# A Griffin and short-convolution block in fp32: split weights kept in DRAM, weight sums moved, operands split sooner, a last product by token tiles

## The chip, the cores and the metric

The kernel runs on one core of a Trainium2 chip. The metric is the device time of one execution in microseconds; 2272.66 us is the median of three runs of the kernel before (2270.35 to 2274.27). A profile of one further execution stands beside them, with its own time. The engines are TensorE (PE, with its weight loads as PEld), VectorE (DVE), ScalarE (ACT), GpSimd (POOL) and SyncE (SP), each with a queue that it works off in order; DMAs are issued here from SP and POOL, and in the changed kernel also from ACT.

## The reference

One layer, sequence 2048, width 1024, all in float32:

```python
h = rmsnorm(x, norm_mix_g)
u = h @ w_in                       # 1024 x 3584, columns: b, c, v (512 each), x_r, g (1024 each)
y_conv = gate_b * causal_dwconv(gate_c * v, conv_w)
xr = causal_dwconv(x_r, rnn_conv_w) + rnn_conv_b
y_rnn = rg_lru(xr, ...) * gelu(g)  # r, i = sigmoid(block-diagonal linear of xr); scan over time
y = concat([rmsnorm(y_conv), rmsnorm(y_rnn)])
x = x + y @ w_out                  # 1536 x 1024
h = rmsnorm(x, norm_mlp_g)
z = square(relu(h @ w_mlp_in))     # 1024 x 4096
x = x + z @ w_mlp_out              # 4096 x 1024
out = rmsnorm(x, final_norm_g)
# rg_lru: a = exp(-8 r softplus(-lambda)); h_t = a h_(t-1) + sqrt(1 - a^2) i xr
```

## The kernel before, in words

**Split operands.** Each fp32 operand of a matmul is split into two fp32r tiles: hi is a copy by ACT (L160), lo the difference by DVE (L161), both in `round_off`. A product takes three matmuls, hi x hi, hi x lo and lo x hi. Every split is thus one ACT and one DVE operation on a tile of 128 x 1024.

**Blocks and pairs.** The 2048 tokens are four blocks of 512, worked off as two pairs. In a pair come the mixers, then w_out for the first and the second block (`po`), then the first MLP product (`Up`), then the second (`Down`).

**Seven products.** From the first MLP product on, the matrix products of a pair are done in Strassen's way: seven quarter products in place of eight, numbered 1 to 7 and run in `ORDER` = 1, 2, 6, 5, 7, 3, 4, each of 24 matmuls (`block_product`, L746, or `Down.multiply`, L1023). Products 1, 2 and 4 (of `w_in`) take quarters of the weight as they are, the others sums of quarters. The mixers of the first pair (`mixers_plain`) are done plainly, since there the quarters are first loaded and split; when a unit's weights have been used, `keep_sums` makes the sums of its group and spills them to DRAM. The second pair's mixers (`mixers_blocks`) fetch for each product one quarter: a sum from DRAM (`wk<-d_wk`), or for 1, 2 and 4 the raw weight from the input (`wk<-in_w_in_dram`), four products ahead, and split it two products ahead.

**The Lru mixers.** The seven groups of columns are four Lru groups (each 256 columns of x_r and of g), two short-convolution groups and the gate b. While the products of group s run, the two units of group s - 1 go through `gate` (the small block-diagonal products `psri` on PE, L492, with two sigmoids on ACT), `scan` and `out`. A unit needs `conv` first: one tensor_scalar (L475) and three more operations on DVE, and a split into xr_hi and xr_lo. `scan` has on DVE L507, L511, L512 (a tensor_scalar, r = v + 1), L513, L515 and the scan L516, on ACT L509, L510 and L514, and a copy of the last state on POOL (L517). `out` has L521 on DVE, a spill of y on POOL's queue and a square on ACT (L526). [...]

**w_out.** `w_out_rows` takes the recurrent part of y, 256 rows at a time, fetched from DRAM and split with the gain by `split_y` (L600 on ACT, L601 on DVE); `w_out_conv` takes the convolution's part, and makes the norm for the MLP with it.

**Up and Down.** `Up` has eight slices of 512 columns with seven products each, 56 in all; operands are prepared two products ahead, results drained from PSUM, squared, combined and spilled as z on SP's queue. `Down` fetches z and w2 from DRAM four products ahead. Its sums of w2's quarters are made once, in the first pair: `w2_sums`, eight times, in the first 16 of Down's 56 products, with four loads, four DVE additions of 128 x 1024 (L976 to L979) and four spills on POOL.

**What sets the order.** In the mixers of the second pair, Up and Down PE's order is the order in which the code is written. The other engines' instructions are placed by a scheduler, and each waits in its own queue for what is ahead of it. Tiles come from pools with a fixed number of slots, 15 for weights (`wp`) and 23 for temporaries (`tp`); a DMA into a slot waits for the slot's last reader.

## Time and profile before

| | us |
|---|---|
| median of three runs | 2272.66 (2270.35 to 2274.27) |
| the profiled execution | 2272.3 |
| its span | 2270.5 |
| mean granted clock of PE | 0.973 |

| stage (us of the span) | length | PE busy | DVE busy | ACT busy | clock | DMA share |
|---|---|---|---|---|---|---|
| 60 to 360, mixers of the first pair | 300 | 300.0 | 209.8 | 154.6 | 1.00 | 0.41 |
| 360 to 520, w_out | 160 | 147.0 | 92.2 | 62.9 | 0.96 | 0.38 |
| 520 to 835, Up | 315 | 313.7 | 226.9 | 108.8 | 0.99 | 0.47 |
| 835 to 960, start of Down | 125 | 114.2 | 90.0 | 46.3 | 0.96 | 1.03 |
| 960 to 1206, rest of Down, first products | 246 | 246.0 | 162.9 | 110.0 | 1.00 | 0.58 |
| 1206 to 1424, Lru mixers of the second pair | 218 | 184.8 | 173.8 | 147.6 | 0.91 | 0.29 |
| 1424 to 1485, other mixers | 61 | 61.0 | 33.9 | 18.6 | 1.00 | 0.58 |
| 1485 to 1675, w_out | 190 | 175.0 | 123.2 | 83.9 | 0.96 | 0.32 |
| 1675 to 2257, Up and Down | 582 | 582.0 | 342.6 | 203.6 | 1.00 | 0.50 |
| 2257 to 2271, the end | 14 | 0.4 | 9.0 | 4.0 | 0.64 | 0.39 |

How to read it: a window's busy times of the engines overlap, so no row adds up to its length; what counts is which of them is missing on PE and what PE was waiting for there. The clock is the share of full speed that the profile shows as granted to PE. A row of waits names the waiting instruction and the instruction that released it, with the total, the number and the longest of the waits; a row of instructions gives line, engine, operation, output and inputs, the shapes, the count, then busy time, mean ns of one, and the idle time of the engine before them.

### The profile page before, as it was taken

The numbers are of one execution on the slowest core, as the hardware profiler recorded it, in microseconds if no ns is written. First come the engines' busy times: TensorE is split into PE (matmuls) and PEld (weight loads), VectorE is DVE, ScalarE is ACT, GpSimd is POOL, SyncE is SP. The second block draws the span as 40 slices with busy tenths as digits, with TensorE's granted clock in tenths as the row PEclk, the third lists the DMA queues.
The fourth block names the chain that finished last, engine by engine and source line by source line (L and its number), as shares of the span: only waits on it lengthen the run. The fifth ranks groups of instructions, "written<-read, shape, count | busy, mean of one in ns | idle before, by whom it ended". The sixth has DMA issues, their size and how long they took to land.

```text
span 2270.5 us, 24706 instructions
## 1 busy us (share of the span) xinstructions
PE 2165.8 (95%) x9514; PEld 1785.4 (79%) x9514; DVE 1505.4 (66%) x1726; ACT 973.6 (43%) x1222; POOL 75.5 (3%) x106
## 2 busy tenths in 40 slices
PE   6999999999999989999998888999999999999997
PEld 5888887787888878788886666877788888888886
DVE  6788744649775767676758778556687666554445
ACT  5576513425323324343546666334343333433433
POOL 0011000000000011000000101000000000000000
PEclk7999999999999999999999899999999999999999
DMA  7333545421543499986342222555115444776441
GB/s 274 130 116 125 167 148 177 162 80 48 200 160 141 160 375 413 417 337 213 131 162 70 90 94 92 175 193 176 47 72 188 158 149 176 290 294 240 158 148 75
DMA packets 174743, 398.58 MB, mean 176 GB/s; under 512 B 12832, under 2 KB 72736, under 8 KB 174624
## 3 DMA queue, kind: packets, MB, share of 16 engines
q1 hardware_dynamic: 164768, 361.33, 44.4%
q0 software_dynamic: 9856, 35.66, 4.0%
q8 instruction: 75, 1.23, 0.2%
q14 instruction: 44, 0.36, 0.0%
HBM read 281.59 MB, written 115.34 MB: 175 GB/s over the span
## 4 chain that ended last, share of the span: by engine, by line
PE 51%; DVE 5%; ACT 1%; issue 1%; DVEq 0%
PE dn L1023 22%; PE up L746 13%; PE in L746 10%; PE po L229 6%; DVE xr L516 1%; DVE w_lo L161 1%; PE psri L492 1%; DVE gi L515 0%; DVE xr L479 0%; DVE H L161 0%; ACT L514 0%; ACT w_hi L160 0%; DVE gi L521 0%; DVE x L1067 0%; ACT xr L514 0%
## 5 line engine op out<-in xcount | busy, mean ns | idle before, releaser
L746 PE MATMUL up<-H,w_hi 128*128 128x512 f32 x1792 | 554.2, 391 | 2.3 <-DVE snap L932 2.3
L161 DVE TENSOR_TENSOR w_lo<-w,w_hi 128x1024 fp32r<-128x1024 f32 x208 | 253.2, 1222 | 266.4 <-ACT w_hi L160 138.0
L746 PEld LDWEIGHTS up<-H,w_hi 128*128 128x128 f32 x1792 | 337.3, 189 | 73.0 <-ACT H L160 3.1
L1023 PE MATMUL dn<-w_lo,z_hi 128*128 128x512 f32 x896 | 350.4, 391 | 9.7 <-DVE w_lo L161 9.7
L746 PE MATMUL up<-H,w_lo 128*128 128x512 f32 x896 | 350.3, 391 | 5.2 <-DVE w_lo L161 5.2
L1023 PE MATMUL dn<-w_hi,z_hi 128*128 128x512 f32 x896 | 349.9, 391 | 0.0
L1023 PE MATMUL dn<-w_hi,z_lo 128*128 128x512 f32 x896 | 349.7, 390 | 0.0
L160 ACT CAST w_hi<-w 128x1024 fp32r<-128x1024 f32 x208 | 215.6, 1049 | 134.3 <-PE dn L1023 117.8
L746 PE MATMUL in<-H,w_hi 128*128 128x512 f32 x784 | 248.4, 399 | 16.2 <-ACT w_hi L160 16.2
L1023 PEld LDWEIGHTS dn<-w_lo,z_hi 128*128 128x128 f32 x896 | 168.9, 188 | 46.8 <-DVE w_lo L161 11.6
L160 ACT CAST z_hi<-z 128x1024 fp32r<-128x1024 f32 x112 | 117.7, 1051 | 200.7 <-PE dn L1023 158.1
L746 PEld LDWEIGHTS up<-H,w_lo 128*128 128x128 f32 x896 | 168.9, 189 | 41.2 <-DVE w_lo L161 6.0
L1023 PEld LDWEIGHTS dn<-w_hi,z_hi 128*128 128x128 f32 x896 | 168.8, 188 | 35.4 <-ACT z_hi L160 0.2
L1023 PEld LDWEIGHTS dn<-w_hi,z_lo 128*128 128x128 f32 x896 | 168.9, 189 | 35.0
L746 PEld LDWEIGHTS in<-H,w_hi 128*128 128x128 f32 x784 | 151.4, 194 | 49.0 <-ACT w_hi L160 17.5
L161 DVE TENSOR_TENSOR z_lo<-z,z_hi 128x1024 fp32r<-128x1024 f32 x112 | 136.8, 1222 | 76.2 <-issue 57.7
L161 DVE TENSOR_TENSOR w_lo<-raw,w_hi 128x1024 fp32r<-128x1024 f32 x76 | 92.8, 1223 | 125.5 <-ACT w_hi L160 84.8
L746 PE MATMUL in<-H,w_lo 128*128 128x512 f32 x392 | 156.5, 399 | 17.0 <-DVE w_lo L161 17.0
L160 ACT CAST w_hi<-raw 128x1024 fp32r<-128x1024 f32 x76 | 79.8, 1051 | 187.1 <-PE po L229 109.7
L229 PE MATMUL po<-w_hi,y_hi 128*128 128x512 f32 x384 | 123.4, 403 | 21.1 <-ACT y_hi L600 21.1
L919 ACT COPY snap<-up 128x1024 f32<-128x1024 f32 x48 | 48.7, 1014 | 193.1 <-PE up L746 193.1
L229 PE MATMUL po<-w_hi,y_lo 128*128 128x512 f32 x384 | 122.1, 400 | 0.7 <-DVE y_lo L601 0.7
(241 smaller groups left out, 3110.7 us busy)
## 6 DMA issues: line engine op xcount, KB each, us to landing
z<-d_z SPq DMA_DIRECT2D x112, 512.0 KB, 7.1
w<-in_w_mlp_out_dram SPq DMA_DIRECT2D x80, 512.0 KB, 9.4
w<-in_w_mlp_in_dram SPq DMA_DIRECT2D x64, 512.0 KB, 4.5
d_z<-snap SPq DMA_DIRECT2D x64, 512.0 KB, 2.6
w<-d_w SPq DMA_DIRECT2D x64, 512.0 KB, 4.6
raw<-in_w_out_dram SPq DMA_DIRECT2D x48, 512.0 KB, 3.5
d_z<-z SPq DMA_DIRECT2D x48, 512.0 KB, 2.6
d_w<-w POOLq DMA_DIRECT2D x32, 512.0 KB, 7.5
```

The source lines that it names most:

```text
L160: nc.scalar.copy(hi, src)
L161: V.tensor_tensor(lo, src, hi.bitcast(F32), SUB)
L229: nc.tensor.matmul(ps[:, half, :], ys[:, j, t * P : (t + 1) * P], ws[j][:, 0, half * 512 : (half + 1) * 512], start=first and i == 0, stop ...
L492: nc.tensor.matmul(ps[g][:, blk, :], ws[:, j, g, :], xs[:, blk * TB : blk * TB + TB], start=i == 0, stop=i == len(pl) - 1,)
L516: V.tensor_tensor_scan(v, r, gi, state[:, c, :], MUL, ADD)
L746: nc.tensor.matmul(ps[:, j, :], ws[:, k, j * P : (j + 1) * P], hs(k), start=i in (1, 2, 5) and k == 0 and n == 0, stop=k == 3 and n == len ...
L919: nc.scalar.copy(t, ps)
L1023: nc.tensor.matmul(ps[t // 2][:, t % 2, :], zs[:, p, t * P : (t + 1) * P], ws[:, p, :], start=i in (1, 2, 5) and a == 0 and p == 0 and n == 0,
```

## The change

- **Split quarters kept.** When a unit of `w_in` is split in the first pair, the hi and lo tiles of quarters 1, 2 and 4 are spilled to DRAM (`spill_r`, L131 of the changed kernel): six DMAs of 512 KB on SP's queue for the first two units, 36 on POOL's for the others. The second pair fetches them as `wr` on POOL's queue (L742), both tiles of a quarter, three products ahead, and does not split these quarters.
- **Lru units.** The first operation of `conv` and r = v + 1 go from DVE to ACT, as Identity with scale and bias (L492, L533). The spill of y goes from POOL's queue to ACT's. The steps of the two units are spread over the products 1, 2, 6, 5 and 7 (`STEPS`); for the first group they start at 6 as before.
- **y.** The split of the first y operand of each block comes sooner (`early`): under the last mixer products for the first block, ahead of `w_out_conv` for the second. `w_out_conv` of the second block is called after the first two preparations of Up.
- **w2's sums** are made in the first pair's Up, after products 8, 11, ... 53, in 16 jobs: two loads of 512 KB with rows of 4 KB, four DVE additions of 128 x 512, four stores on POOL's queue, with the tiles from the weights' pool.
- **The end.** The last two products of the second pair's Down are run token tile by token tile, half of the squares of the final norm are made before, each tile is finished behind its matmuls, with its two stores on SP's and ACT's queues. The other outputs go out on POOL's queue.
- The diagonal matrices for the second pair's scale are made at product (6, 1) of Down, three products sooner.

ACT's queue in the third Lru group of the second pair, first before, then changed; CAST is the hi half of a split, L501/L522 and L502/L523 are the sigmoids, L510/L531 exp, L514/L535 sqrt, L765/L789 the copy of product 6 out of PSUM, L475/L492 the first operation of the convolution:

```order
L526 ACTIVATE xr<-gi 128x1024
L160 CAST w_hi<-wk 128x1024 x2
L765 COPY xr_in<-in 128x2x512
L501 ACT_TABLE_LOAD
L501 ACTIVATE r<-psri,prm 128x1024
L502 ACTIVATE gi<-psri,prm 128x1024
L509 ACTIVATE xr<-r,sp_323 128x1024
L510 ACT_TABLE_LOAD
L510 ACTIVATE r<-r,sp_324 128x1024
L160 CAST xr_hi<-xr 128x1024
```

```order
L523 ACTIVATE gi<-psri,prm 128x1024
L492 ACTIVATE xr<-xr_in,prm 128x1024
L530 ACTIVATE xr<-r,sp_335 128x1024
L531 ACT_TABLE_LOAD
L531 ACTIVATE r<-r,sp_336 128x1024
L789 COPY xr_in<-in 128x2x512
L533 ACTIVATE r<-xr,ones 128x1024
L166 CAST xr_hi<-xr 128x1024
L166 CAST w_hi<-wk 128x1024
L535 ACT_TABLE_LOAD
```

The first unit's sigmoids now stand ahead of the copy of product 6, and that copy and L533 stand ahead of the second unit's xr_hi; the casts of products 1 and 2 (`x2` behind L526) are gone.

ACT's queue where the second pair's mixers end and w_out begins, before and changed; L811/L835 copy a gate product out of PSUM, L600/L621 are the hi half of a y operand, L526/L547 a square of the convolution's output:

```order
L811 COPY snap<-in 128x1024
L160 CAST w_hi<-raw 128x1024 x3
L526 ACTIVATE q<-u 128x1024 x2
L160 CAST w_hi<-raw 128x1024
L526 ACTIVATE q<-u 128x1024 x2
L600 ACTIVATE y_hi<-y,prm 128x512 x8
```

```order
L835 COPY snap<-in 128x1024
L621 ACTIVATE y_hi<-y,prm 128x512 x2
L166 CAST w_hi<-raw 128x1024 x3
L547 ACTIVATE q<-u 128x1024 x2
L166 CAST w_hi<-raw 128x1024
L547 ACTIVATE q<-u 128x1024 x2
L166 CAST w_hi<-raw 128x1024 x2
L621 ACTIVATE y_hi<-y,prm 128x512 x6
```

The first two of the eight halves have moved ahead of the squares, which wait for the last mixer product.

DVE's queue in the first pair's Up, changed; w_lo is the lo half of a weight, L974 and L953 drain and square a product, L977 to L990 make the sums of z, L1007 to L1010 are the additions of one w2 job:

```order
L974 TENSOR_TENSOR snap<-up,snap 128x1024
L167 TENSOR_TENSOR w_lo<-w_4341,w_hi 128x1024
L953 SCALAR_TENSOR_TENSOR snap<-snap 128x1024
L937 TENSOR_TENSOR w_4341<-w_4341 128x1024
L977 TENSOR_TENSOR z_4650<-snap 128x1024
L167 TENSOR_TENSOR w_lo<-w_4341,w_hi 128x1024
L979 TENSOR_TENSOR snap<-snap 128x1024
L1007 TENSOR_TENSOR w_4699<-w_4699,w_4698 128x512
L982 TENSOR_TENSOR z_4657<-snap 128x1024
L1008 TENSOR_TENSOR w_4698<-w_4698 128x512
L990 TENSOR_TENSOR z_4694<-snap,z_4657 128x1024
L1009 TENSOR_TENSOR w_4698<-w_4698,w_4699 128x512
```

The four additions of a job are new in this queue and stand among the drains and the lo halves.

The diff at its core:

```diff
 ORDER = (1, 2, 6, 5, 7, 3, 4)
+STEPS = {1: (0,), 2: (1,), 6: (2,), 5: (3,), 7: (4,)}
...
 
+    def spill_r(nm, t, queue):
+        d = dp.tile(list(t.shape), F32, name="d_" + nm)
+        queue.dma_start(d, t.bitcast(F32))
+        return d
+
...
         n = units[u][3]
+        pairs = [split_new(r, wtile, "w") for r in rs]
...
             rawkept.setdefault(n, []).extend(rs)
-        splits[u] = tuple(zip(*[split_new(r, wtile, "w") for r in rs]))
+            f = u % 2
+            for half, i in ((0, 1), (1, 2)) if f == 0 else ((1, 4),):
+                kept[n, i] = [spill_r("ws", t, nc.sync if u < 2 else nc.gpsimd) for t in pairs[half]]
+        splits[u] = tuple(zip(*pairs))
...
             xr = self.new("xr", (P, 2 * TB))
-            V.tensor_scalar(
-                xr, xin[:, j, 0 : 2 * TB], par("rnn_conv_w", c), par("rnn_conv_b", c), MUL, ADD
+            nc.scalar.activation(
+                xr,
+                xin[:, j, 0 : 2 * TB],
+                AF.Identity,
+                bias=par("rnn_conv_b", c),
+                scale=par("rnn_conv_w", c),
...
             V.scalar_tensor_tensor(v, r, 1.0, v, ADD, MUL)
-            V.tensor_scalar(r, v, 1.0, None, ADD)
+            nc.scalar.activation(r, v, AF.Identity, bias=ones[:, 0:1])
...
             acc = add_sq(acc, self.y, self.v)
-            return spill("y", self.y, nc.gpsimd), acc
+            return spill("y", self.y, nc.scalar), acc
...
             u = us[pr]
+            if pr == 1:
+                early = split_y(fetched[0], "g_norm_rnn", 0)
...
         keep_sums(6)
-        return us, ysB, acc, rB, fetched
+        return us, ysB, acc, rB, fetched, early
...
         def fetch(self, i):
+            ds = kept.pop((self.n, i))
             if i in (1, 2, 4):
-                f = i // 4
-                t = wtile("wk", WSHAPE)
-                load(t, halves(w_in, GROUPS[self.n][1 + 2 * f])[i // 2 if i < 4 else 1])
+                self.ready[i] = [wtile("wr", WSHAPE, F32R) for _ in range(2)]
+                for t, d in zip(self.ready[i], ds):
+                    nc.gpsimd.dma_start(t, d)
             else:
-                t = refill("wk", kept.pop((self.n, i)), wtile)
-            self.raw[i] = t
+                self.raw[i] = refill("wk", ds, wtile)
...
         def prepare(self, i):
-            self.ready[i] = split_new(self.raw.pop(i), wtile, "w")
+            if i in self.raw:
+                self.ready[i] = split_new(self.raw.pop(i), wtile, "w")
...
         for n in range(-FETCHW, len(seq)):
-            m = n + FETCHW
-            if m < len(seq):
-                G[seq[m][0]].fetch(seq[m][1])
+            for m, sums in ((n + FETCHW, True), (n + FETCHW - 1, False)):
+                if 0 <= m < len(seq) and (seq[m][1] not in (1, 2, 4)) == sums:
+                    G[seq[m][0]].fetch(seq[m][1])
...
                 p = G[s - 1]
-                if i == 6:
-                    p.units[0].gate(p.gw)
-                    p.units[1].conv(p.xin)
-                    p.units[0].scan()
-                    y, acc = p.units[0].out(p.g, acc)
-                    ysB.append(y)
-                if i == 7:
-                    p.units[1].gate(p.gw)
-                    p.units[1].scan()
-                    y, acc = p.units[1].out(p.g, acc)
-                    ysB.append(y)
+                for step in ({6: (0,), 5: (1, 2), 7: (3, 4)} if s == 1 else STEPS).get(i, ()):
+                    if step == 0:
+                        p.units[0].gate(p.gw)
+                        p.units[1].conv(p.xin)
+                    elif step == 1:
+                        p.units[0].scan()
+                    elif step == 2:
+                        p.units[1].gate(p.gw)
+                        y, acc = p.units[0].out(p.g, acc)
+                        ysB.append(y)
+                    elif step == 3:
+                        p.units[1].scan()
+                    else:
+                        y, acc = p.units[1].out(p.g, acc)
+                        ysB.append(y)
...
                 fetched = [fetch_y(ysB, pr, 0) for pr in range(2)]
+            if s == 6 and i == 7:
+                early = split_y(fetched[0], "g_norm_rnn", 0)
...
         accA = conv_out(G[5].u, accA)
-        return G[6].us, ysB, accA, rB, fetched
+        return G[6].us, ysB, accA, rB, fetched, early
...
 
-    def w2_sums(a):
-        v = w2_quarters(a)
-        t = dict(zip((12, 22, 11, 21), quad("w2", (P, 2, TB))))
-        for nm in (12, 22, 11, 21):
-            load(t[nm], v[nm])
-        b11, b12, b21, b22 = (t[n] for n in (11, 12, 21, 22))
+    def w2_sums(job):
+        a, p = job // 2, job % 2
+        v = w2[512 * a : 512 * a + 512, :].rearrange("(f j p) n -> j p f n", p=P, f=2)[p]
+        ts = [wtile("w2", (P, D)) for _ in range(2)]
         tt = V.tensor_tensor
+        b11, b21, b12, b22 = (t[:, e * TB : e * TB + TB] for e in range(2) for t in ts)
+        for f in range(2):
+            load(ts[f], v[:, f])
...
         for i, t in ((7, b22), (5, b12), (6, b11), (4, b21)):
-            W2[a, i] = spill("w2", t, nc.gpsimd)
+            if p == 0:
+                W2[a, i] = dp.tile([P, 2, TB], F32, name="d_w2")
+            nc.gpsimd.dma_start(W2[a, i][:, p], t)
...
 
-    def finish_tile(b, t, gfin):
-        ss = small("ss")
+    def finish_squares(b, t, ss, dhs):
+        for i in dhs:
+            sq = temp("sq", (P, TB))
+            nc.scalar.activation(sq, x_half(b, t, i), AF.Square, accum_out=ss[:, i : i + 1])
+
+    def finish_tile(b, t, gfin, ss=None, queues=None):
         rs = small("rs")[:, 0:1]
-        sq = temp("sq")
-        for i in range(2):
-            nc.scalar.activation(
-                sq[:, i], x_half(b, t, i), AF.Square, accum_out=ss[:, i : i + 1]
-            )
+        if ss is None:
+            ss = small("ss")
+            finish_squares(b, t, ss, range(2))
+        else:
+            finish_squares(b, t, ss, (0,))
...
             V.scalar_tensor_tensor(xv, xv, rs, gfin[:, sl], MUL, MUL)
-            nc.sync.dma_start(outf[r0 : r0 + P, sl], xv)
+            (queues or (nc.gpsimd, nc.gpsimd))[i].dma_start(outf[r0 : r0 + P, sl], xv)
...
 
-    def w_out_rows(b, ysB, rB, ys, during):
+    def w_out_rows(b, ysB, rB, ys, during, early):
...
                 ys.append(fetch_y(ysB, pr + 2, blk))
-            y = split_y(ys[pr], "g_norm_rnn", 2 * pr)
+            y = early if pr == 0 else split_y(ys[pr], "g_norm_rnn", 2 * pr)
...
         if b == 0:
-            us, ysB, accA, rB, fetched = mixers_plain(h)
+            us, ysB, accA, rB, fetched, early = mixers_plain(h)
...
             with tc.manual_schedule(engines={nc.tensor.engine}):
-                us, ysB, accA, rB, fetched = mixers_blocks(ops.H, finish_operands)
+                us, ysB, accA, rB, fetched, early = mixers_blocks(ops.H, finish_operands)
...
         raw0 = [temp("raw0") for _ in range(4)]
-        w_out_rows(b, ysB, rB, fetched, lambda pr: None)
+        w_out_rows(b, ysB, rB, fetched, lambda pr: None, early)
...
         fetched = [fetch_y(ysB, pr, 1) for pr in range(2)]
+        early = split_y(fetched[0], "g_norm_rnn", 0)
...
         with tc.manual_schedule(engines={nc.tensor.engine}):
-            xs = w_out_conv(b + 1, ysA, rA, 1, rest)
...
             for n in range(-LEAD1, len(seq)):
+                if n == 0:
+                    xs = w_out_conv(b + 1, ysA, rA, 1, rest)
...
                     ups[1].load((0,))
+                    ups[2].load((0,))
...
                 ups[s].drain(i, Z)
+                if more and n > 7 and n % 3 == 2:
+                    w2_sums(n // 3 - 2)
                 if n == 0:
-                    ups[2].load((0,))
...
             R = None
-            for n in range(len(dseq)):
+            for n in range(len(dseq) - (0 if more else 2)):
...
                 if more:
-                    if n < 16 and n % 2 == 0:
-                        w2_sums(n // 2)
...
                         ops2 = Operands()
+                    if (i, a) == (6, 1):
+                        diags = [diagonal(rs_next[:, k, :], NT) for k in range(2)]
...
                         for k in range(2):
-                            nc.scalar.copy(bcs[k], spread(rs_next[:, k, :], NT))
+                            nc.scalar.copy(bcs[k], spread(rs_next[:, k, :], NT, diags[k]))
...
                         ops2.put(ops2.begin(5), r0[:2])
-        finish(b + 1)
+            if not more:
+                gfin = gain(final_norm_g)
+                ends = [small("ss") for _ in range(NT)]
+                for t in range(NT):
+                    finish_squares(b + 1, t, ends[t], (1,))
+                for t in range(NT):
+                    for i, a in dseq[-2:]:
+                        down.multiply(i, a, (t,))
+                    xv = x_half(b + 1, t, 0)
+                    V.tensor_add(xv, down.x[t // 2][:, t % 2], xv)
+                    finish_tile(b + 1, t, gfin, ends[t], (nc.sync, nc.scalar))
         if more:
+            finish(b + 1)
```

More of the change, by code (lines that the diff above doesn't have):

```diff
@@ L160, in round_off @@
         nc.scalar.copy(hi, src)
-        V.tensor_tensor(lo, src, hi.bitcast(F32), SUB)
+        latest[0] = V.tensor_tensor(lo, src, hi.bitcast(F32), SUB).ins
+    latest = [None]
     def split_new(src, new, nm):
@@ L344, in norm_rows, with diagonal @@
         return rs
-    def spread(rs, n):
+    def diagonal(rs, n):
         diag = temp("diag", (P, n, P))
@@ L349, in spread @@
             V.tensor_scalar(diag[:, k, :], ident, rs[:, k : k + 1], None, MUL)
+        return diag
+    def spread(rs, n, diag=None):
+        if diag is None:
+            diag = diagonal(rs, n)
         ps = psum("bc", (P, n * P))
@@ L1202, in during @@
                 ups[0].load((0,))
-        w_out_rows(b + 1, ysB, rB, fetched, during)
+        w_out_rows(b + 1, ysB, rB, fetched, during, early)
         raw1 = [temp("raw1") for _ in range(4)]
```

## The prediction

> **What bounds the kernel now.** I read the page's first part, then PE's waits over the whole run, then windows around the waits.
>
> ```profile
> PE 2165.8 (95%) x9514; PEld 1785.4 (79%) x9514; DVE 1505.4 (66%) x1726; ACT 973.6 (43%) x1222; POOL 75.5 (3%) x106
> ...
> PE po L229 <- ACT y_hi L600: 21.1, 4, 5.6
> PE in L746 <- DVE w_lo L161: 17.0, 4, 8.4
> PE in L746 <- ACT w_hi L160: 16.2, 3, 5.4
> PE bc L351 <- DVE diag L349: 11.5, 3, 9.6
> PE dn L1023 <- DVE w_lo L161: 9.7, 3, 6.9
> PE up L746 <- DVE w_lo L161: 5.2, 2, 2.6
> PE up L746 <- DVE snap L932: 2.3, 2, 1.2
> ```
>
> PE is busy 95% of the time and computes the same products afterwards, so a gain can only come from its gaps and from what follows them. The waits (total, times, longest) add up to 83 us in a few places, and PE does not come out of a long one at full clock:
>
> ```profile
> 960.00:1206.00 246.00, 246.00 (x1087) 203.71 (x1085) 162.85 (x201) 109.97 (x142) 0.55 (x1) 1.00 0.58 205
> 1206.00:1424.00 218.00, 184.76 (x768) 149.45 (x767) 173.79 (x149) 147.63 (x141) 22.57 (x19) 0.91 0.29 94
> 362.00:378.00 16.00, 11.07 (x37) 8.44 (x36) 11.23 (x13) 8.13 (x11) 0.00 (x0) 0.79 0.58 197
> 440.00:456.00 16.00, 10.37 (x34) 7.71 (x33) 13.48 (x23) 12.17 (x26) 0.70 (x2) 0.79 0.91 325
> 1485.00:1500.00 15.00, 9.40 (x29) 6.98 (x29) 12.29 (x14) 9.29 (x13) 0.00 (x0) 0.77 0.59 195
> 1563.00:1580.00 17.00, 11.37 (x41) 8.63 (x40) 13.80 (x24) 12.50 (x27) 1.01 (x2) 0.80 0.90 319
> 517.00:525.00 8.00, 5.42 (x19) 4.03 (x18) 7.96 (x19) 5.99 (x16) 1.06 (x2) 0.79 0.33 133
> 1640.00:1650.00 10.00, 7.42 (x28) 5.66 (x27) 9.96 (x24) 6.14 (x16) 1.07 (x2) 0.83 0.26 107
> 835.00:850.00 15.00, 8.10 (x24) 6.37 (x24) 11.41 (x10) 2.00 (x2) 2.13 (x4) 0.66 1.02 411
> ```
>
> The columns are the window, its length, busy time and count on PE, weight load, DVE, ACT and POOL, then granted clock, DMA share and GB/s. The first row has no gap and gives the price of a matmul: 246 / 1087 = 0.2263 us, so a product of 24 takes 5.43 us. What a window loses is its length minus its matmuls at that price. The second pair's Lru mixers lose 218 - 768 x 0.2263 = 44.2 us, although the PE waits there are 17.0 + 16.2 = 33.2: the other 11 are half clock after the gaps. The four starts of a w_out product (`po`) lose 7.6 + 8.3 + 8.4 + 7.7 = 32.0 us, the two starts of the first MLP product 3.7 each, the start of the second MLP product 9.6.
>
> **The change part by part.** *Mixers.* One group of the second pair lies in 1260 to 1314:
>
> ```profile
> 1260.00:1314.00 54.00, 45.57 (x190) 36.73 (x190) 42.41 (x37) 37.22 (x36) 5.88 (x5) 0.91 0.30 93
> ...
> L161 DVE TENSOR_TENSOR w_lo<-wk,w_hi 128x1024 fp32r<-128x1024 f32 x7 | 8.5, 1220 | 3.5 <-ACT w_hi L160 3.4
> L160 ACT CAST w_hi<-wk 128x1024 fp32r<-128x1024 f32 x7 | 7.2, 1048 | 3.9 <-PE in L746 2.6 <-DVE xr L529 1.3
> L517 POOL COPY state<-xr 128x1 f32<-128x1 f32 x2 | 4.3, 2162 | 37.0 <-DVE xr L516 37.0
> L501 ACT ACT_TABLE_LOAD x2 | 2.6, 1283 | 0.0
> L161 DVE TENSOR_TENSOR xr_lo<-xr,xr_hi 128x1024 fp32r<-128x1024 f32 x2 | 2.4, 1222 | 0.0
> L526 ACT ACTIVATE xr<-gi 128x1024 f32<-128x1024 f32 x2 | 2.1, 1060 | 5.7 <-POOL state L517 5.6
> L160 ACT CAST xr_hi<-xr 128x1024 fp32r<-128x1024 f32 x2 | 2.1, 1040 | 0.0
> L475 DVE TENSOR_SCALAR xr<-xr_in,prm 128x1024 f32<-128x1024 f32 x2 | 1.6, 812 | 0.7 <-PE in L746 0.7
> L512 DVE TENSOR_SCALAR r<-xr 128x1024 f32<-128x1024 f32 x2 | 1.4, 686 | 0.0
> L765 ACT COPY xr_in<-in 128x1024 f32<-128x1024 f32 x1 | 1.0, 1014 | 4.4 <-PE in L746 4.4
> ```
>
> DVE works 42.4 us for a group whose 192 matmuls need 43.5 us. A queue that full can't catch up after a wait for psri or for the scan. The change takes three w_lo (3 x 1.22), two L475 (2 x 0.81) and two L512 (2 x 0.69) off it: 42.4 - 6.7 = 35.7 us, 82%. ACT loses three w_hi (3 x 1.05), and gets four operations of about 1.06 (priced by L526, the same tile) and, by the order of the built program, one more table load (1.28): 37.2 - 3.1 + 4.2 + 1.3 = 39.6 us, 91%. So ACT becomes the fuller queue, though what PE needs from it falls from seven casts to four.
>
> [...]
>
> I walked the new order of a group by hand with these durations. In the groups behind the first and the third Lru group ACT stands in a copy of a PSUM tile that waits for the end of a product, with xr_hi behind it, and the psri that needs xr_hi is next on PE: 1.01 + 1.04 + the exposed part of xr_lo (1.22) = 3.3 to 4, with the L512 that has moved to ACT ahead of it about 4.3. The other two stall about 1.1 and 0.6 us. With 2.6 us of half clock after each of the two long ones (PE's 45.57 less 190 x 0.2263 in the group above) 4.0 + 1.1 + 4.3 + 0.6 + 5.2 = 15 us remain of 44: **gain 29**. Bounds: 12 (if ACT's queue falls behind in every group as DVE's does now) and 42. The fetches of the split quarters are twice the bytes of three of seven; DMA share is 0.30 there, and they are issued 3 to 4 products (16 to 21 us) ahead on POOL's queue, behind state copies that end early enough: 0.
>
> *First y operand.* The split is issued a product earlier. Its ACT and DVE operations (2 x about 0.63 and 0.75) fall under that product, where PE is never waiting. po then needs w_hi/w_lo of w_out, which are split a unit ahead. **Gain 30** of 32.0; bounds 16 (only the block whose split moves under `b1` or the last mixer product) and 32.
>
> *Start of the first MLP product.* The last w_out product goes behind two weight preparations. The two windows lose 7.4 us and the snap waits 2.3; DVE's queue stays full (7.96 of 8 us), so not all goes: **gain 6**, bounds 2 and 9.7.
>
> *w2's sums.* They leave the second MLP product: 9.6 us in the window above and the rest of the dn row, 9.7 - 6.9 = 2.8. **Gain 12**, bounds 9.6 and 12.4 (all three dn waits lie in the first pair's; the second pair's Down, without these sums, has none). The bc row has 11.5 - 9.6 = 1.9 us beside its wait at the very start; the larger of its two other waits (1.2) lies at the diagonals that are now made three steps sooner: **gain 1**. The sums now come as 16 jobs, one per three products (16.3 us) of Up, each with two loads of 512 KB on SP, four additions of half length on DVE (0.69 each, by the 128x512 gate row below) and four stores on POOL:
>
> ```profile
> 520.00:835.00 315.00, 313.67 (x1383) 259.22 (x1383) 226.91 (x223) 108.75 (x129) 4.26 (x8) 0.99 0.47 173
> ...
> L161 DVE TENSOR_TENSOR gate<-gate_raw,gate 128x512 fp32r<-128x512 f32 x1 | 0.7, 690 | 0.0
> ...
> w<-in_w_mlp_out_dram SPq DMA_DIRECT2D x6, 512.0 KB, 4.9
> ...
> w<-in_w_mlp_out_dram SPq DMA_DIRECT2D x28, 512.0 KB, 13.5
> d_w<-w POOLq DMA_DIRECT2D x24, 512.0 KB, 7.5
> ...
> d_y<-gi POOLq DMA_DIRECT2D x8, 512.0 KB, 3.0
> ```
>
> DVE is busy 72% of Up. 16 x 4 x 0.69 = 44 us more over 250 us make 90% there. The harder limit is a chain. In the built program several jobs' loads wait for the stores of the job before, since they take its buffers, and DVE, in order, waits for the loads with w_lo of the next products behind. In calm rows a job is 4.9 (load) + 4 x 0.69 and three other operations between them of 1.22 (6.4) + 0.5 (issue) + 3.0 (store) = 14.8 us, below 16.3; in the rows of the crowded Down start (share 1.02) 13.5 + 6.4 + 0.5 + 7.5 = 27.9. The share in Up goes from 0.47 to about 0.8 (33.6 MB over 250 us are 134 GB/s more, less the quarter of them that ran there already), so I stand nearer the calm row: single jobs late by 1 to 4 us, part of it covered because operands are prepared two products ahead. **Cost 8**, bounds 0 and 100 (the rivals below).
>
> *Start.* Six spills of 512 KB go on SP's queue ahead of the loads of x and x_t for the second block.
>
> ```profile
> 0.00:60.00 60.00, 41.75 (x192) 35.57 (x193) 41.25 (x95) 33.45 (x61) 1.65 (x11) 0.77 0.72 259
> L356 DVE SCALAR_TENSOR_TENSOR xT<-xT,prm,bcs x8: 746/748/751, 49.1 to 56.0; 128x512 f32<-128x512 f32 x8
> L121 SPq DMA_DIRECT2D xT<-in_x_t_dram x8: 434/792/2133, 2.2 to 22.0; - x8
> ```
>
> 3.1 MB at 411 GB/s are 7.7 us. The x_t loads are issued by 22 us and first used at 49; late by the spills and by the three raw loads now ahead of them, they land at about 46 to 52. **Cost 2**, bounds 0 and 8. The other 36 spills of the first pair run on POOL's queue at a share of 0.4, issued right after each split, a product or more before their buffers are wanted: 0.
>
> *Tail.* The chain of waits after the last matmul (start, length, what):
>
> ```profile
> 2257.46 1.22 DVE x L1037
> ...
> 2263.65 1.33 DVE x L1067 x2
> ...
> 2265.84 0.66 DVEq L1375
> ```
>
> PE ends at 2257.4, the span at 2270.5: 13.1 us, of which 4.7 are the last store. By token tiles only the last tile stands behind PE: one addition (0.7), one square (0.6), the small operations (0.9), L1067 (1.33), the store (4.7) = 8.2; a slip of 0.4 because a tile's finish fills DVE about as long as its 12 matmuls (2.72 us). **Gain 4.5**, bounds 2 and 6.
>
> **Sum:** 29 + 30 + 6 + 12 + 1 + 4.5 - 8 - 2 = 72.5 us. The profiled execution took 2272.3 us (span 2270.5 and 1.8 around it), and 2272.3 - 72.5 = 2199.8; the median of the runs, 2272.66, lies 0.4 above it: **2200 us**.
>
> **The rivals.**
> (a) *ACT takes DVE's place in the mixers.* It is 91% full, in order, and its copies wait for PE. The gain there is 12 instead of 29: 2217. For it: L526 waited 5.6 us in the group above for a POOL copy, and still precedes casts. Against it: three of seven casts need ACT no more.
> (b) *The w2 chain is a little longer than three products*, 18 us: each job then costs 1.7 us, 16 x 1.7 = 27 in place of 8: 2219. For it: the landing times grow with the share; against it: about half of the loads wait for PE or a z store and not for the job before.
> (c) *The same chain decides the run, slower than before.* At x us beyond 16.3 each job stalls PE x, and from about 2.5 on the clock halves, as after the 2.6 us wait at 1640 (clock 0.83 over 10 us, 1.7 us lost). To lose the whole 80.5 us (72.5 without the 8) takes 80.5 / 16 = 5.0 us per job, that is x = 3.3 and a chain of 19.6. At the middle of the two sums, 21.3, x is 5.0 and the loss 16 x (5.0 + 2.9) = 126: 2318 (2.9 is what the y gaps lose after their 5 us). Against it: the share of 1.02 that makes 27.9 is not reached.
> [...]
> (d) *Nearly every stall goes*: mixers 42, y 31, first MLP 9.7, w2 12.4, diagonal 1, tail 6, Up and the start 1: 101 us, 2172. For it: each change has its own stall. Against it: the walk of ACT's order above.
>
> **Chances.** Forecast (2183 to 2214) 0.55, (a) 0.15, (b) 0.14, (d) 0.09, (c) 0.05, no effect beyond 0.2% 0.02. The range 2174 to 2240 takes in (a), (b), most of (d) and mixtures; the forecast's own is 2183 to 2214. Runs of the kernel before spread over 0.17%, so 0.2% (4.5 us) is about what can be told. Faster 0.93, same 0.02, slower 0.05.
>
> **What would show it.** The PE waits `po <- y_hi` and `dn <- w_lo` vanish (right for 42 us); the window of the Lru mixers is near 189 us long, with waits on xr_hi or xr_lo at psri, not on w_hi. In Up the wait of L1007 for its load is short and PE's row of waits there below 8 us; long ones with the clock below 1 there mean (b) or (c). The tail is about 8.6 us. I am wrong if Up is longer than before, or if the mixers' window still has waits on w_hi behind L547.

## The result and the profile after

The changed kernel takes 2209.22 us (median of four runs, 2208.02 to 2210.33), the kernel before 2272.78 in the same comparison: a ratio of 0.9721, with an interval of 0.9704 to 0.9738. 63.6 us are gone where 72.5 were forecast.

The page's first part and PE's waits over the whole run of the changed kernel (waiting, releaser: total, times, longest):

```profile
PE 2148.5 (97%) x9514; PEld 1773.1 (80%) x9514; DVE 1461.3 (66%) x1707; ACT 996.3 (45%) x1239; POOL 129.0 (6%) x224
...
PE bc L368 <- DVE diag L361: 10.0, 2, 9.3
PE psri L513 <- ACT xr_hi L166: 8.3, 3, 3.1
PE psri L513 <- DVE xr_lo L167: 7.7, 7, 2.4
PE up L770 <- DVE w_lo L167: 3.9, 1, 3.9
PE po L241 <- ACT y_hi L621: 3.5, 2, 1.8
PE up L770 <- DVE snap L962: 3.4, 2, 1.7
...
PE in L770 <- DVE w_lo L167: 2.4, 2, 1.4
...
PE ps_v L222 <- ACT gc L702: 1.7, 1, 1.7
PE dn L1056 <- DVE x L1371: 1.6, 2, 0.8
...
PE dn L1056 <- DVE w_lo L167: 0.4, 1, 0.4
```

The waits of `in` on w_hi (16.2 us) are gone, `po` on y_hi fell from 21.1 to 3.5, `dn` on w_lo from 9.7 to 0.4. The four waits of `in` on w_lo (17.0 us) have become two (2.4 us). In their place stand waits that the kernel before did not have: `psri` on xr_hi and xr_lo, 16 us, and two of `dn` on L1371, the addition in the tiled end. `up` waits once for w_lo, 3.9 us in the middle of the first pair's Up, where the kernel before waited 2.6 us at the start of each Up.

The stages of the changed kernel in the same columns as before:

```profile
60.00:368.00 308.00, 301.92 (x1335) 248.82 (x1334) 199.91 (x193) 182.30 (x199) 36.17 (x51) 1.00 0.56 195
368.00:507.00 139.00, 137.13 (x633) 113.73 (x632) 88.95 (x157) 58.74 (x108) 3.20 (x6) 1.00 0.43 148
507.00:823.00 316.00, 310.25 (x1372) 256.33 (x1371) 255.10 (x284) 108.92 (x132) 35.63 (x66) 0.99 0.69 251
823.00:1130.00 307.00, 306.58 (x1349) 252.99 (x1348) 185.50 (x200) 127.48 (x150) 8.56 (x16) 1.00 0.64 234
...
1184.00:1378.00 194.00, 179.97 (x762) 145.51 (x762) 151.94 (x124) 152.00 (x143) 24.22 (x37) 0.97 0.41 138
1378.00:1441.00 63.00, 63.00 (x287) 52.46 (x286) 31.01 (x41) 16.71 (x19) 3.37 (x7) 1.00 0.67 225
1441.00:1583.00 142.00, 140.14 (x643) 116.15 (x642) 91.31 (x160) 60.95 (x113) 3.20 (x6) 0.99 0.39 137
```

At 0.2263 us a matmul the second pair's Lru mixers now lose 194 - 762 x 0.2263 = 21.6 us where they lost 44.2. Up has DVE busy 81% (72% before) and a DMA share of 0.69 (0.47). The first pair's mixers were without a wait from 60 us on; now PE is busy 301.9 of 308 us there.

| ledger by the ends of the stages in the two traces, us | before | after | gained |
|---|---|---|---|
| to the last product of the first pair's mixers | 362.6 | 367.7 | -5.0 |
| from there to the last `po` of the first pair | 153.6 | 139.3 | 14.3 |
| Up, first pair | 313.2 | 315.5 | -2.3 |
| Down, first pair | 321.2 | 307.1 | 14.1 |
| mixers, second pair | 334.5 | 311.7 | 22.8 |
| `po`, second pair | 154.3 | 140.9 | 13.4 |
| Up, second pair | 313.1 | 309.3 | 3.8 |
| Down, second pair, and the end | 318.1 | 316.2 | 1.8 |

The column sums to 62.9 us, the difference of the two spans (2270.5 and 2207.7).

### The profile page after: what moved, and what is told of

Its sections match the earlier page's. It is cut to its first block, busy times and chain, and to the rows that moved or that the text cites. A ratio compares the mean times of both kernels' runs of the same rounds, so it can differ in the third digit from the quotient of the medians.

```text
span 2207.7 us, 24962 instructions
## 1 busy us (share of the span) xinstructions
PE 2148.5 (97%) x9514; PEld 1773.1 (80%) x9514; DVE 1461.3 (66%) x1707; ACT 996.3 (45%) x1239; POOL 129.0 (6%) x224
## 5 line engine op out<-in xcount | busy, mean ns | idle before, releaser
L770 PE MATMUL in<-H,w_hi 128*128 128x512 f32 x448 | 138.7, 391 | 0.0
L241 PE MATMUL po<-w_lo,y_hi 128*128 128x512 f32 x384 | 119.1, 392 | 0.0
L770 PE MATMUL in<-H,wr 128*128 128x512 f32 x504 | 116.0, 390 | 0.0
```

Of the source, the lines that this page charges most:

```text
L241: nc.tensor.matmul(ps[:, half, :], ys[:, j, t * P : (t + 1) * P], ws[j][:, 0, half * 512 : (half + 1) * 512], start=first and i == 0, stop ...
L770: nc.tensor.matmul(ps[:, j, :], ws[:, k, j * P : (j + 1) * P], hs(k), start=i in (1, 2, 5) and k == 0 and n == 0, stop=k == 3 and n == len ...
```

## The experiments

All kernels are the changed kernel with one edit, unless the text says more. Each ratio is to the kernel before, measured beside it; the changed kernel's own is 0.9721.

**1. The convolution's start back on DVE in the first pair.**

```diff
-            nc.scalar.activation(xr, xin[:, j, 0 : 2 * TB], AF.Identity, bias=..., scale=...)
+            if self.new is wtile:          # the second pair
+                nc.scalar.activation(xr, xin[:, j, 0 : 2 * TB], AF.Identity, bias=..., scale=...)
+            else:
+                V.tensor_scalar(xr, xin[:, j, 0 : 2 * TB], ..., MUL, ADD)
...
(the same for r = v + 1)
```

> The changed kernel, with the first convolution operation and r = v + 1 back on DVE in the first pair alone (the second pair keeps them on ACT). Theory C: in the changed kernel's first pair psri waits for xr_hi and xr_lo (2.1 + 1.0 + 1.4 us, and 1.7 us of ps_v on a copy by ACT) because the convolution's first operation stands in ACT's queue behind casts and copies; with it on DVE these waits go, the stage from 60 to 368 us is 6 to 7 us shorter, and the run takes about 2203 us. Rival S: the 42 spills of split quarters hold buffers and queues there; then the waits stay and the time stays within 2 us of 2209.

Measured: 2201.04 us, ratio 0.9681 (0.9664 to 0.9697). No psri and no ps_v waits before 360 us; the mixers' last product ends at 359.7 us and not at 367.7. Theory C stands as far as it goes: with the two operations back on DVE, xr_hi is in time. (Experiment 2 shows what else it takes.) PE's waits on psri in this kernel, all of them in the second pair:

```profile
PE psri L518 <- ACT xr_hi L166: 6.2, 2, 3.1
PE psri L518 <- DVE xr_lo L167: 5.1, 5, 2.4
```

**2. Quarters fetched raw and split, nothing kept.**

```diff
-                kept[n, i] = [spill_r("ws", t, nc.sync if u < 2 else nc.gpsimd) for t in pairs[half]]
...
-                self.ready[i] = [wtile("wr", WSHAPE, F32R) for _ in range(2)]
-                for t, d in zip(self.ready[i], ds):
-                    nc.gpsimd.dma_start(t, d)
+                t = wtile("wk", WSHAPE)
+                load(t, halves(w_in, GROUPS[self.n][1 + 2 * f])[i // 2 if i < 4 else 1])
```

> The changed kernel without the kept quarters: no spills of hi and lo in the first pair, and quarters 1, 2 and 4 fetched raw and split in the second pair, as before; the operations on ACT and the steps stay. Theory A (the fullness of DVE's queue made the stalls): three splits of 1.22 us per group return, DVE is at 39.4 and ACT at about 41 of 43.5 us per group, and the Lru mixers of the second pair lose 15 to 22 us more than the changed kernel's 22: 2224 to 2231 us. Rival O (the order of the steps and the place of psri made the gain): at most 6 us longer there, 2209 to 2215. Rival S of the first pair: the waits on psri there vanish without the spills, and 6 us come off.

Measured: 2210.74 us, ratio 0.9717 (0.9702 to 0.9731): no different from the changed kernel. Two things cancel. The mixers of the second pair take 317.8 us from their first product to their last, the changed kernel 311.8: 6 us more. The first pair's last mixer product ends at 361.6 us, 6 us sooner, without a psri wait, although the convolution starts on ACT there too. So in the first pair it takes both, the operation on ACT and the spills, before the built order puts xr_hi behind the copy of g; rival S and theory C were both half right. Theory A's 15 us did not come; with the new places of the steps the kept quarters are worth 6 us in the mixers, and they cost as much in the first pair.

**3. The convolution's start and r = v + 1 back on DVE in the second pair.**

```diff
+            if self.new is not wtile:      # the first pair
+                nc.scalar.activation(...)
+            else:
+                V.tensor_scalar(...)
```

> The changed kernel with the first convolution operation and r = v + 1 back on DVE in the second pair alone (the first pair keeps them on ACT). By the prediction's sum DVE gets 3.0 us more per group (35.7 to 38.7 of 43.5) and ACT 4.2 less. Theory D (DVE's fullness is what counts): the four groups together lose 4 to 10 us more, 2213 to 2219 us. Rival (a) of the prediction (ACT is now the queue that PE waits for, xr_hi stands behind a copy and r = v + 1): the long waits of psri on xr_hi (3.1 us twice, with half clock after them) shrink, and the run is 4 to 8 us shorter, 2201 to 2205.

Measured: 2213.67 us, ratio 0.9730 (0.9716 to 0.9745); the mixers take 314.8 us (311.8). The intervals overlap, so the runs tell no difference; the 3 us of the trace are below theory D's 4 to 10, and rival (a)'s gain did not come. PE's waits on psri:

```profile
PE psri L518 <- ACT xr_hi L166: 10.8, 4, 4.5
PE psri L518 <- DVE xr_lo L167: 5.0, 6, 1.5
```

The wait on xr_hi grows (8.3 to 10.8 us) although ACT has less to do. In the longest, which ends at 1199.0 us, DVE has xr ready at 1194.6, and ACT runs a copy of g, a table load and exp before it casts xr_hi at 1197.9: the order in ACT's queue makes this wait, not how full the queue is. That speaks against rival (a) of the prediction. It does not settle it, since the edit also gave DVE more to do; experiment 4 says more.

**4. The steps back at their old places.**

```diff
-                for step in ({6: (0,), 5: (1, 2), 7: (3, 4)} if s == 1 else STEPS).get(i, ()):
+                for step in {6: (0, 1, 5), 7: (2, 3, 4)}.get(i, ()):
...
                     elif step == 2:
                         p.units[1].gate(p.gw)
+                    elif step == 5:
                         y, acc = p.units[0].out(p.g, acc)
```

> The changed kernel with the two units' steps where they were before: psri, scan and output of the first unit after product 6, of the second after product 7; kept quarters and the operations on ACT stay. Rival O (the order made the gain): 8 to 15 us longer, with waits of products 1 and 2 of the next group, 2217 to 2224 us. Theory A (the queues' fullness did it): within 4 us of 2209, since no splits of products 1 and 2 can be late any more, and the waits on xr_hi at psri may even go, because psri stands later than xr_hi.

Measured: 2189.24 us, ratio 0.9624 (0.9610 to 0.9639), 20 us faster than the changed kernel. Neither range held: rival O's loss of 8 to 15 us did not come, and theory A's 2209 within 4 us was too cautious. One whole Lru group in this kernel:

```profile
1231.00:1274.50 43.50, 43.50 (x193) 35.94 (x192) 37.08 (x30) 38.12 (x38) 5.90 (x9) 1.00 0.43 151
```

PE is busy for all of the 43.5 us, with DVE at 85% and ACT at 88%. The whole mixer stage takes 290.4 us and has no wait above 0.5 us. The casts of xr_hi end 1.7 to 11.7 us before the eight psri steps that need them; in the changed kernel it is 0.1 to 3.1 us. So the new places of the steps, which were part of the change, cost 21 us; the rest of the change gave all the mixers could give.

**5 and 6. Old places without the kept quarters, and old places with the two operations on DVE** (the edit of 4 with that of 2, and with that of 3).

> The changed kernel with the steps where they were and without the kept quarters (raw fetch and split of 1, 2 and 4, no spills); the operations on ACT stay. Together with the earlier runs this asks what is needed beside the old places of the steps, with which the changed kernel's mixers of the second pair ran in 290 us without a wait. Theory Q (kept quarters are needed: without them DVE is at 39.4 of 43.5 us and w_hi stands behind the squares that wait for the scan): the mixers lose 15 to 30 us again, 2200 to 2215 us. Rival E (the operations on ACT alone are enough): no waits in the mixers, and 6 us less in the first pair because psri's waits there went with the spills: 2180 to 2185 us.

> The changed kernel with the steps where they were and, in the second pair, the first convolution operation and r = v + 1 on DVE; kept quarters stay. Theory Q (kept quarters alone are enough with the old steps): no waits in the mixers, 2187 to 2192 us as with the operations on ACT. Rival E (the operations on ACT are needed): 10 to 25 us lost in the mixers, 2199 to 2214 us.

Measured: 2211.65 us, ratio 0.9733 (0.9717 to 0.9749), and 2196.74 us, ratio 0.9660 (0.9645 to 0.9674). Without the kept quarters the old waits are back:

```profile
PE in L767 <- ACT w_hi L166: 14.2, 3, 5.5
...
PE in L767 <- DVE w_lo L167: 5.2, 4, 4.5
```

With the operations on DVE only short ones stay (the 1.5 us lie in the first pair):

```profile
PE psri L518 <- DVE xr_lo L167: 3.9, 5, 1.5
...
PE in L778 <- DVE w_lo L167: 2.8, 4, 0.8
```

Both theories Q and E were too simple: at the old places the kept quarters are worth 30 us and the operations on ACT 8, and only with both are there no waits. The three parts together, by the length of the second pair's mixers (first to last product; the whole runs also hold what happens in the first pair):

| steps at | quarters | operations on | mixers, us | whole run, us |
|---|---|---|---|---|
| old places | raw | DVE | 334.7 | (the kernel before) |
| old places | raw | ACT | 320.6 | 2211.7 |
| old places | kept | DVE | 298.5 | 2196.7 |
| old places | kept | ACT | 290.4 | 2189.2 |
| new places | raw | ACT | 317.8 | 2210.7 |
| new places | kept | DVE | 314.8 | 2213.7 |
| new places | kept | ACT | 311.8 | 2209.2 (the change) |

The first row lacks the other parts of the change too. The new places with raw quarters and the operations on DVE were not run.

**7. Only the second unit's psri one product later.**

```diff
-STEPS = {1: (0,), 2: (1,), 6: (2,), 5: (3,), 7: (4,)}
+STEPS = {1: (0,), 2: (1,), 5: (2,), 7: (3, 4)}
...
-                for step in ({6: (0,), 5: (1, 2), 7: (3, 4)} if s == 1 else STEPS).get(i, ()):
+                for step in ({6: (0,), 5: (1,), 7: (2, 3, 4)} if s == 1 else STEPS).get(i, ()):
```

The first unit's output goes with that step, and the second unit's scan goes from product 5 to 7.

> The changed kernel with only the second unit's psri (and the first unit's output, its square and its spill, which go with that step) one product later in every Lru group of the second pair: after product 5 in place of 6, in the first group after 7 in place of 5. Theory P (each long wait is psri standing one product too early for an xr_hi that is queued behind the copy of the product just run): the waits on xr_hi of 3.1 us twice, the xr_lo waits of 0.8 and 1.0 us right behind them and their half clock go, 11 to 14 us, 2195 to 2198 us; the waits at the first unit's psri, which keeps its place, stay. Rival N (any later psri only moves the wait into the next group's products, as in the kernel before): less than 5 us off, above 2204.

Measured: 2213.90 us, ratio 0.9737 (0.9721 to 0.9753): rival N. PE's waits:

```profile
PE in L770 <- ACT w_hi L166: 12.8, 3, 4.8
...
PE psri L513 <- ACT xr_hi L166: 3.1, 2, 2.0
```

The long waits at psri are gone as theory P said (the 3.1 us left lie in the first pair), but three of 4.0 to 4.8 us stand at the products. ACT's queue before the one that ends at 1288.9 us (start, length, operation, and in brackets the idle time before it):

```profile
1284.94 1.01 ACT L789 COPY xr_in<-in 128x1024 f32<-128x1024 f32 x1 [1.04 <-PE in L770]
1285.85 1.15 ACT L533 ACTIVATE r<-xr,ones 128x1024 f32<-128x1024 f32 x1
1286.90 1.03 ACT L166 CAST xr_hi<-xr 128x1024 fp32r<-128x1024 f32 x1
1287.83 1.04 ACT L166 CAST w_hi<-wk 128x1024 fp32r<-128x1024 f32 x1
```

The copy waits for the end of the product before, and r = v + 1 and xr_hi stand between it and the weight of the next product. With psri later, PE no longer waits for xr_hi, and now waits for the cast queued right behind it. The other two waits have xr_hi and r = v + 1 ahead of the weight in the same way.

**8. The w2 jobs after every second product.**

```diff
-                if more and n > 7 and n % 3 == 2:
-                    w2_sums(n // 3 - 2)
+                if more and 8 <= n < 40 and n % 2 == 0:
+                    w2_sums(n // 2 - 4)
```

> The changed kernel with the 16 jobs of w2 after every second product of Up (8, 10, ... 38) and not after every third. The prediction's theory: load, additions and store of one job make a chain that the next job waits for, of 14.8 us at the least. In the changed kernel DVE waited 17.6 us in 8 of 16 jobs for a load. With 10.9 us to a job the chain sets the pace: 16 x (14.8 - 10.9) = 62 us at most, less what the two products of lead cover, so Up is 25 to 60 us longer, 2234 to 2270 us. Rival: half of the jobs don't wait for the one before, and DVE's load (7.8 + 2.8 of 10.9 us) still fits: Up within 8 us, 2205 to 2217 us.

Measured: 2230.51 us, ratio 0.9809 (0.9794 to 0.9823). Up takes 338.4 us and not 314.9, 24 more, just under what the theory expected. DVE begins the first addition of the 16 jobs between 569.4 and 761.8 us, 12.8 us apart, where two products are 10.9 and my least chain was 14.8. But the jobs are issued behind products that are slowed themselves, so the 12.8 us don't measure the chain. SP's loads wait for the stores of w2 sums 24.9 us in the changed kernel's Up (8 times) and not at all in this one: that a job's loads wait for the stores of the job before is not what slows it. DVE's wait for the loads in Up is hardly longer than the changed kernel's 17.6 us:

```profile
DVE w L1007 <- DMA w<-in_w_mlp_out_dram: 18.3, 7, 5.4
```

What is longer is the wait of ACT's weight casts for the stores, first in the changed kernel, then in this one:

```profile
ACT w_hi L166 <- DMA d_w<-w: 17.4, 5, 11.5
```

```profile
ACT w_hi L166 <- DMA d_w<-w: 30.6, 6, 7.3
```

The jobs' tiles come from the pool of the weights, so a cast can wait for a tile that is still being stored. PE has 13.8 us of waits on w_lo in `up` here, and the clock over Up is 0.96 (0.99 in the changed kernel). Which of these waits sets the pace was not separated.

**9. The first y operand split at its old places.**

```diff
-                early = split_y(fetched[0], "g_norm_rnn", 0)
...
-            y = early if pr == 0 else split_y(ys[pr], "g_norm_rnn", 2 * pr)
+            y = split_y(ys[pr], "g_norm_rnn", 2 * pr)
```

> The changed kernel with the first y operand of each block split where it was before (inside w_out, after the mixers' last operations and after w_out_conv). Theory Y: the four waits of po on y_hi return (4.9 to 5.6 us each) with about 3 us of half clock behind each, less the two of 1.8 us that stand in the middle of w_out now: 25 to 30 us longer, 2234 to 2240 us. Rival W (another part, such as the w_out weights' order, removed the waits): less than 10 us, below 2219.

Measured: 2237.35 us, ratio 0.9843 (0.9828 to 0.9858): 28 us longer, theory Y.

```profile
PE po L241 <- ACT y_hi L621: 21.1, 4, 5.6
```

The row is the one of the kernel before, to the tenth.

**10. The sums of w2 back in Down** (`w2_sums` and its call as in the kernel before).

> The changed kernel with the sums of w2 back in the first 16 products of Down, as before. By the prediction's terms Down loses 12.4 us again, and Up gets back what the jobs cost it there, in the changed kernel's trace one wait of 3.9 us with 1.7 us of half clock: 6 to 8 us longer in all, 2215 to 2218 us. Rival: DVE's load in Up cost more than its one wait shows (Up is 316 us with the jobs), or Down's crowding stays away because the finished rows went elsewhere: no longer than the changed kernel, 2209 or less.

Measured: 2219.45 us, ratio 0.9763 (0.9746 to 0.9779): 10 us longer, a little more than expected. Down takes 318.8 us (307.3), Up 310.8 (314.9), so the jobs cost Up 4 us.

**11 and 12. Two versions from what was seen.** The first has the steps at the old places (4), the first pair's operations on DVE (1), the second y operand split early as well, the last product's token tiles in the order 0, 2, 1, 3, and the w2 loads one product sooner; the second has all of that but the last.

```diff
-                early = split_y(fetched[0], "g_norm_rnn", 0)
+                early = [split_y(fetched[k], "g_norm_rnn", 2 * k) for k in range(2)]
...
-                for t in range(NT):
+                for t in (0, 2, 1, 3):
                     for i, a in dseq[-2:]:
```

> A version from what was seen so far: the changed kernel with the steps where they were (20 us), the first pair's convolution start and r = v + 1 on DVE (8 us), the token tiles of the last product in the order 0, 2, 1, 3 so that a tile does not wait for the reader of its PSUM neighbour (two waits of 0.8 us), the w2 loads issued one product sooner (one stall of 3.9 us and 1.7 us of half clock after it), and the second y operand split early too (two waits of 1.8 us, with 1.7 us of half clock each). Sum: 20 + 8 + 1.6 + 5 + 5 = 40 us off 2209: 2169 us, between 2165 and 2182. Rival: two more temporaries and two more weight tiles held make new waits for slots, 2182 or more.

> The version z2_best without the earlier issue of the w2 loads. In z2_best the stall in Up did not go, it moved (one wait of 4.8 us in place of 3.9 us), since the load still waits for a weight buffer. If buffers are what the loads wait for, giving up the earlier issue costs nothing: 2171 to 2175 us. Rival: the earlier issue helped other jobs, and without it Up is 3 to 6 us longer: 2177 to 2180 us.

Measured: 2174.08 us, ratio 0.9562 (0.9548 to 0.9577), and 2173.30 us, ratio 0.9562 (0.9547 to 0.9576). All of PE's waits in the second that are left:

```profile
PE bc L368 <- DVE diag L361: 10.0, 2, 9.3
PE up L778 <- DVE w_lo L167: 4.1, 1, 4.1
PE up L778 <- DVE snap L971: 3.4, 2, 1.7
PE ps_x L222 <- ACT h_hi L166: 3.3, 1, 3.3
PE start_x L396 <- ACT w_hi L166: 2.2, 1, 2.2
PE start_x L385 <- POOL ones L252: 1.1, 1, 1.1
PE up L778 <- DVE snap L979: 0.5, 1, 0.5
PE ps_x L222 <- DVE h_lo L167: 0.2, 1, 0.2
```

Apart from the start, some 9 us of waits remain. This version is 36 us faster than the changed kernel (0.9562 against 0.9721). Issuing the w2 loads sooner gave nothing; the one stall in Up only moved.

## Why the prediction was right, and where not

The direction and the size hold (63.6 us for 72.5, in the range). Step by step:

- *Mixers, gain 29: 22.6 measured.* The walk left 10.0 us of waits and 5.2 of half clock. The trace has 14.0 us of waits in nine places, and a clock of 0.50 from 1196.4 to 1199.7 us and from 1288.6 to 1295.3, some 5 us lost. Of the two long stalls the one at 1288 us came as walked, behind the copy of product 6 and r = v + 1: 3.1 + 1.0 us for 4.3. The one at 1195 us has the size, 3.1 + 0.8 us for 4.0, and another cause. The convolution's first operation stood on ACT behind a table load and the first unit's sigmoids and ended at 1189.6, so xr itself was late on DVE (start, length):

```profile
1189.65 3.92 DVE L500 SCALAR_TENSOR_TENSOR xr<-xr_in,prm,xr 128x1024 f32<-128x1024 f32 x3
...
1193.29 0.99 ACT L792 COPY g<-in 128x1024 f32<-128x1024 f32 x1
1194.18 1.04 ACT L166 CAST xr_hi<-xr 128x1024 fp32r<-128x1024 f32 x1
```

The copy there does not wait for a product and delays the cast by 0.6 us only. The short stalls were 2.4 + 0.5 and 0.8 us for 1.1 and 0.6, and two waits of `in` on w_lo (1.0 and 1.4) were not in the walk.

- *The steps' new places, not priced by themselves.* I walked only the new order, and not the new parts in the old order. The 15 us that I left over I took for the price of ACT's queue; experiment 4 shows them to be the price of the steps' new places. ACT at 88% and DVE at 85% run without any wait at the old places. That "A queue that full can't catch up", said of DVE at 42.4 of 43.5 us, is neither shown nor refuted: with raw quarters at the old places (experiment 5) a group has 40.9 us of work on DVE and 40.5 on ACT, and the waits are back.
- *Rival (a)*, ACT in DVE's place, has the symptom (waits on xr_hi) and not the cause: what counts is what stands ahead of xr_hi on ACT (experiments 3 and 4).
- *Table loads.* The prediction counts one load more at the 1.28 us of its row, whose 0.0 is the idle time before a load. Behind each of the eight loads of that group the trace has 0.01 to 0.02 us of idle time, so the 1.28 us stand. In the kernel before the loads, 1.28 us each, stand ahead of sigmoids, exp, sqrt and gelu; the 16 tanh (L509) ran without one of their own.
- *Spills at 0, and the convolution's start on ACT in the first pair not priced at all.* This is the term that was missing: 8 us (experiment 1), and it takes the spills as well (experiment 2). Without it the first pair's mixers end at 359.7 us, 2.9 us sooner than in the kernel before, so the start shows no cost where I put 2. PE's granted clock in the first 60 us is not the same from run to run (0.77 in the kernel before, 0.94 in the changed kernel), so how much of that is the start can't be told.
- *First y operand, gain 30:* 28 (experiment 9). What is left are two waits of 1.8 us for the second operand.
- *Start of Up, gain 6, and the w2 jobs, cost 8:* together -2.3 us in the first pair by the ledger, +3.8 in the second, 1.5 for my -2. The jobs cost 4 (experiment 10), half of what I put, so the start gave about 1.7 + 3.8 = 5.5.
- *w2 out of Down and the diagonal, gain 13:* 14.1.
- *The tail, gain 4.5:* 1.8. The time after PE fell from 13.1 to 9.1 us, for 8.6 expected, but Down itself became 2.2 us longer to its last matmul. What the sum lacked is that a token tile's matmuls wait for the addition that reads its neighbour in the same PSUM tile (1.6 us). In the order 0, 2, 1, 3 (experiments 11 and 12) the two waits are gone, Down is 2.2 us shorter again and the time after PE 0.4 to 0.6 longer.

The tail's chain in the changed kernel shows that wait twice:

```profile
2184.80 3.41 PE dn L1056 x15
2188.21 0.02 issue
2188.23 0.70 DVE x L1371
2188.94 0.04 issue
2188.98 5.79 PE dn L1056 x24
2194.77 0.03 issue
2194.80 0.70 DVE x L1371
2195.50 0.04 issue
2195.54 3.05 PE dn L1056 x12
```

- *Rivals (b) and (c)*, the chain of the w2 jobs: in the changed kernel the loads do wait for the stores of w2 sums (8 times, 24.9 us), but the jobs keep the pace of the products, 16.4 us apart, and one late load reached PE (3.9 us). How long the chain is at its least no run shows.
- *The signs.* The prediction called itself wrong if Up is longer than before. The first pair's Up is, by 2.3 us, as its own cost of 8 for the jobs against a gain of 6 for the start implied; over both pairs Up is 1.5 us shorter. No `in` waits for w_hi any more.

Most terms fell short: the mixers by 6 us, y by 2, the tail by 3, the first pair by 3. That the jobs cost 4 us less than forecast took part of this off again, and so much of the result is luck.

## What to carry over

A change of several parts should be walked with each part at its old and its new value: here one part, steps put earlier, cost 21 us in the same mixers in which the other two gained 44, and the sum still looked like a success. Queues at 85 and 88% made no stall in experiment 4; look at what stands ahead of the operand that PE wants next, and at what that waits for. When an operation moves to another engine, it moves at all its call sites, those included where nothing was waiting before.

## What the runs showed of the hardware

The same wait did not cost the same clock. In the changed kernel PE waits 1.76 us for the second y operand at 378.5 us and again at 1452.1 us, with the same instructions on both sides:

```profile
376.00:390.00 14.00, 12.13 (x53) 9.43 (x52) 6.43 (x8) 5.79 (x8) 0.00 (x0) 1.00 0.77 266
...
1450.00:1465.00 15.00, 13.14 (x50) 10.09 (x49) 6.43 (x8) 5.79 (x8) 0.00 (x0) 0.89 0.81 280
```

Behind the first the clock stays at 1.00; behind the second it falls, the mean of the 15 us is 0.89, that is 0.11 x 15 = 1.7 us lost. A longer wait, 2.38 us for xr_lo from 1222.9 us on, left it at 1.00 (1225.2 to 1228 us). So the 2.5 us from which rival (c) has the clock halve is an estimate of mine from one wait of 2.6 us, and no limit that these traces show; the 1.7 us that the expectation of experiment 11 puts behind each of the two y waits came behind the second alone. What decides the clock behind a wait no row shows.
